# Full-height operands in a convolution's transforms, split products with the late part last, and a transposition moved one block on

## The chip, the core and the metric

The kernel runs on one core of a Trainium2 chip. The core has five engines with an instruction stream each: TensorE (PE) multiplies matrices of up to 128 rows into PSUM, VectorE (DVE) and ScalarE (ACT) work element by element, GpSimd (POOL) works element by element more slowly and issues gathers, and SyncE (SP) issues most DMA transfers. Streams run in order and wait for each other by semaphores. The metric is the device time of one launch in microseconds (us); less is better. What is shown of a kernel's inside comes from one profiled execution. "PEld" is TensorE's loading of the stationary operand, which precedes each product.

## The reference

One encoder layer on 512 tokens of width 1024, in float32, batch 1:

```python
def rmsnorm(x, g): ...                     # x / rms(x) * g
h = x + hybrid_mixer(rmsnorm(x))
h = h + peer_ffn(rmsnorm(h))
out = rmsnorm(h)
```

The mixer projects the normed tokens to ten blocks of 1024 columns and runs two branches. Branch A is a gated linear recurrence (HGRN2) over 8 heads, forward and backward, each head with a 128 x 128 state: `S_t = diag(f_t) S_{t-1} + k_t v_t^T, o_t = S_t^T q_t`, then a norm and an output gate. Branch B is a convolution:

```python
def bidirectional_fftconv(u, h_fwd, h_bwd, bias):
    L = u.shape[1]                         # 512
    kern = jnp.concatenate([h_fwd, jnp.zeros_like(h_fwd[:1]), h_bwd[1:][::-1]], axis=0)
    uf = jnp.fft.rfft(u, n=2 * L, axis=1)
    kf = jnp.fft.rfft(kern, n=2 * L, axis=0)
    return jnp.fft.irfft(uf * kf[None], n=2 * L, axis=1)[:, :L] + u * bias
```

with `u = v * x1` behind a short convolution of width 3, and `h_fwd`, `h_bwd` made by a small network of positions, `sin(...) @ filt_w3`, times a decaying window. Both branches are projected, gated, added and projected again. The channel mixer (PEER) forms 8 queries of 256 values a token, scores them against two sets of 128 sub-keys each, takes the 16 best of the sums, and for these 16 of 16,384 experts a head adds `softmax * gelu(x . u_e) * v_e`.

## The kernel before

**Split products.** Products that need accuracy are made from two parts of each operand, a high part (a cast to the type fp32r on ACT) and a low part (source minus high part, on DVE or POOL): `split`, lines 83 to 86. `mm3` (L89 to L95) then issues three products for each pair of 128-row blocks: high x high (L93), high x low (L94) and low x high (L95), block after block. In the rows of the profile, `whi`, `wlo` are a weight block's parts, `xh`, `xl` those of the normed tokens, `uh`, `ul` those of a row of the experts' table; the first operand of `mm3` is the stationary one. The low part is made from the high part, so it is there last.

**Order.** The code is written against a layer that records instructions, finds their dependencies, and then lists each engine's instructions by its own schedule of costs and readiness. The written order sets priorities; `issue_after` adds an edge. `weave(main, fill, per)` advances `fill` by a step each time the numbers that `main` yields have summed to `per`.

**Stages.** Norm and transposition of the tokens (to about 20 us); the convolution, `hyena`; its projection with gates; the recurrence, `hgrn`; output projections; queries and selection of experts (`queries`, `select`, `gates_out`); the expert loop (`rows`).

**Convolution.** Channels go in four passes of 256. A pass projects `x1`, `v`, `x0` for two blocks of 128 channels, forms `u`, folds it about its middle row into a sum and a difference (`sd`) and transposes these (L439). The middle row, one value per channel, is brought over by a product with one output row (L444): `pm[:1] = uj[:, H].T @ ident`. The FFTs are products with cosine and sine matrices: `ft` (L393 to L399) makes two blocks with `mm3` and adds the middle row by one further product, `alt` times `um` or `fm` (L399). These one-row operands are tiles of 33 rows: the high part in row 0, the low part in row 32, zeros between (`one_row`, `split_row`). `nyquist` (L404 to L406) makes one row of output, and the way back adds its own one-row product (L545, `YN` and `alt`). The filter's last layer is `hid2` (128 rows: 64 high, 64 low) times `fw3h` (L470) plus 64 rows of `hid2` times `fw3l` (L471), for four blocks a pass; then window, fold and split into `f0`, `f1` on DVE and ACT.

**Recurrence.** For each head, `scores` (main) is woven with the next head's projections (`project`, four blocks of 24 products; fill) at `per` 6.0, 5.2 for the last head. `scores` makes running sums `Z` of the gates' logarithms, exponentials `E0`, `EZ`, then transposes keys (L680), multiplies them with values (L686) and adds states `S` on DVE; seven levels follow, each with two subtractions (L707, L708), an exponential on ACT (L709), three products on DVE (L710 to L712), a score product on PE (L716) and a predicated copy (L717). Between heads ACT changes tables for sigmoids and back for the logarithm `lf`, on which the next `Z` (L646) depends.

**Expert loop.** `act_row` (one of 128 blocks of experts) splits a row of the table and issues 24 products into `ps_a`; buffers for `uh`, `ul` are two each. In the loop its low part is made by POOL. `combine` accumulates into `acc`.

## Time and profile before

| | |
|---|---|
| median of 3 runs | 2172.9 us (2167.37 to 2174.68) |
| the profiled execution's own time | 2161.79 us |
| its span, first to last instruction | 2160.0 us |
| granted TensorE clock, mean | 0.991 |
| PE busy | 2087.8 us, 97% |
| DVE busy | 1721.2 us, 80% |
| ACT busy | 967.1 us, 45% |
| POOL busy | 635.4 us, 29% |

A row of a group reads: line, engine, operation, output and inputs by the program's names, stationary and moving shapes, count; then busy time, mean ns of one, and idle time of the engine just before, with what ended it. A product's shape `33*128 33x256` is a stationary operand of 33 rows and 128 columns and a moving one of 33 rows and 256 columns. In a timeline each row begins with its start and its duration in us, and brackets give idle time before it and what ended that. Products overlap in PE's pipeline, so the distance from start to start tells what one costs; its duration is longer. A float32 product (not fp32r) of the program is two records.

### The profile page before, as it was taken

What the parts mean: (1) busy time and instruction counts of PE and PEld (TensorE: products, weight loads), DVE (VectorE), ACT (ScalarE), POOL (GpSimd) and SP (SyncE); (2) the same over time, 40 slices, a digit from 0 to 9 for tenths busy, and PEclk for the clock granted to TensorE, in tenths of its full rate; (3) what the DMA queues carried; (4) which work ended last, traced back from release to release, by engine and by line L of the source; (5) the groups of instructions that cost most, each with busy time, mean ns of one, the idle gap of its engine ahead of it and who ended that gap; (6) DMA issues with size and microseconds to landing.
All of it is one profiled execution on the core that took longest, in us unless ns stands there. A gap on an engine that the chain in (4) does not pass through costs nothing.

```text
span 2160.0 us, 29749 instructions
## 1 busy us (share of the span) xinstructions
PE 2087.8 (97%) x11117; PEld 1827.0 (85%) x11117; DVE 1721.2 (80%) x3073; ACT 967.1 (45%) x1382; POOL 635.4 (29%) x361
## 2 busy tenths in 40 slices
PE   7999999999999999988989999999999999999998
PEld 6777778888888889778889899998998998998997
DVE  6777763799989664999999978878788778877874
ACT  5544442666676532235767523333333333333233
POOL 0000000000000000000000487777677677577650
PEclk9999999999999999999999999999999999999999
DMA  5212113212222263213455699888888888879864
GB/s 192 80 49 57 46 50 111 69 59 59 72 66 59 79 205 127 69 37 120 182 215 211 228 340 342 301 315 318 284 326 323 297 306 326 311 276 325 309 246 146
DMA packets 153661, 406.89 MB, mean 188 GB/s; under 512 B 12425, under 2 KB 65419, under 8 KB 151852
## 3 DMA queue, kind: packets, MB, share of 16 engines
q1 hardware_dynamic: 109884, 255.59, 35.2%
q0 software_dynamic: 36864, 134.23, 17.0%
q10 hardware_dynamic: 6768, 15.17, 2.1%
q8 instruction: 87, 1.43, 0.3%
q14 instruction: 58, 0.48, 0.1%
HBM read 372.83 MB, written 32.11 MB: 187 GB/s over the span
## 4 chain that ended last, share of the span: by engine, by line
PE 75%; DVE 16%; ACT 5%; issue 2%; DMA 1%; POOL 0%; ACTq 0%; DVEq 0%; POOLq 0%
PE acc L971 8%; PE acc L972 8%; PE acc L970 8%; PE ps_a L95 7%; PE ps_a L93 7%; PE ps_a L94 7%; PE ps_mm L94 6%; PE ps_mm L93 6%; PE ps_mm L95 6%; PE ps_g L1226 2%; DVE wlo L86 2%; PE ps_x L93 1%; PE ps_x L716 1%; PE ps_x L95 1%; PE ps_x L94 1%
## 5 line engine op out<-in xcount | busy, mean ns | idle before, releaser
L86 POOL TENSOR_TENSOR ul<-uraw,uh 128x1024 fp32r<-128x1024 f32 x100 | 263.9, 2639 | 608.0 <-DMA gt<-Gd 403.4
L95 PE MATMUL ps_a<-pxh,ul 128*128 128x384 f32 x1008 | 344.2, 342 | 10.4 <-DVE ul L86 6.9
L93 PE MATMUL ps_a<-pxh,uh 128*128 128x384 f32 x1008 | 344.2, 341 | 10.2 <-ACT gact L863 8.3
L94 PE MATMUL ps_a<-pxl,uh 128*128 128x384 f32 x1008 | 341.9, 339 | 0.0
L85 ACT CAST vh<-vraw 128x1024 fp32r<-128x1024 f32 x128 | 134.6, 1052 | 431.5 <-DMA vraw<-in_v 333.3
L972 PE MATMUL acc<-vh,gl 128*128 128x512 f32 x768 | 300.7, 392 | 0.0
L971 PE MATMUL acc<-vl,gh 128*128 128x512 f32 x768 | 300.5, 391 | 0.0
L970 PE MATMUL acc<-vh,gh 128*128 128x512 f32 x768 | 298.7, 389 | 0.0
L931 DVE SCALAR_TENSOR_TENSOR xg<-grow,gw,xg 128x1024 f32<-128x1024 f32 x127 | 206.7, 1628 | 73.0 <-DMA grow<-in_v,gidx 71.3
L922 DVE SCALAR_TENSOR_TENSOR grow<-grow,xg 128x1024 f32<-128x1024 f32 x128 | 200.5, 1585 | 75.4 <-DMA grow<-in_u,gidx 75.1
L93 PE MATMUL ps_mm<-xh,whi 128*128 128x512 f32 (+1 forms) x656 | 257.6, 393 | 3.1 <-ACT gt L238 1.4
L95 PE MATMUL ps_mm<-xh,wlo 128*128 128x512 f32 (+1 forms) x656 | 256.0, 391 | 4.2 <-DVE wlo L86 4.2
L94 PE MATMUL ps_mm<-xl,whi 128*128 128x512 f32 (+1 forms) x656 | 256.9, 392 | 0.3 <-DVE xl L194 0.3
L824 POOL IOTA iota<- 128x512 bf16 x1 | 1.2, 1235 | 791.3 <-DVE gt L279 791.3
L93 PEld LDWEIGHTS ps_a<-pxh,uh 128*128 128x128 f32 x1008 | 192.4, 191 | 15.5 <-ACT gact L863 9.4
L902 POOL DMA_INDIRECT grow<-in_u,gidx x128 | 195.4, 1527 | 32.5 <-issue 23.1
L95 PEld LDWEIGHTS ps_a<-pxh,ul 128*128 128x128 f32 x1008 | 192.1, 191 | 12.7 <-DVE ul L86 8.6
L94 PEld LDWEIGHTS ps_a<-pxl,uh 128*128 128x128 f32 x1008 | 192.3, 191 | 3.8
L85 ACT CAST whi<-wraw 128x1024 fp32r<-128x1024 f32 x112 | 117.5, 1049 | 162.9 <-PE ps_mm L94 131.4
L86 DVE TENSOR_TENSOR vl<-vraw,vh 128x1024 fp32r<-128x1024 f32 x128 | 176.3, 1380 | 12.4 <-ACT vh L85 12.2
L902 POOL DMA_INDIRECT grow<-in_v,gidx x128 | 174.7, 1365 | 37.6 <-issue 17.8
L85 ACT CAST uh<-uraw 128x1024 fp32r<-128x1024 f32 x128 | 134.5, 1051 | 99.9 <-PE ps_a L94 71.5
(413 smaller groups left out, 4260.7 us busy)
## 6 DMA issues: line engine op xcount, KB each, us to landing
uraw<-in_uT SPq DMA_DIRECT2D x128, 512.0 KB, 6.5
vraw<-in_v SPq DMA_DIRECT2D x128, 512.0 KB, 5.6
wraw<-in_w_in SPq DMA_DIRECT2D x80, 512.0 KB, 3.6
Gd<-Gs SPq DMA_DIRECT2D x12, 2048.0 KB, 7.3
gt<-Gd SPq DMA_DIRECT2D x32, 768.0 KB, 8.9
wraw<-in_w_q SPq DMA_DIRECT2D x16, 512.0 KB, 3.7
wraw<-in_w_b SPq DMA_DIRECT2D x8, 512.0 KB, 3.6
wraw<-in_w_a SPq DMA_DIRECT2D x8, 512.0 KB, 4.0
```

The source lines that it names most:

```text
L85: nc.scalar.copy(hi, src)
L86: return (eng or nc.vector).tensor_sub(lo, src, hi).ins
L93: nc.tensor.matmul(out, ah, bh, start=(i == 0), stop=False)
L94: nc.tensor.matmul(out, ah, bl, start=False, stop=False)
L95: nc.tensor.matmul(out, al, bh, start=False, stop=(stop and i == n - 1))
L902: nc.gpsimd.indirect_dma_start(out=t, out_offset=None, in_=tab, in_offset=bass.IndirectOffsetOnAxis(ap=gidx[:, j : j + 1], axis=0))
L922: nc.vector.scalar_tensor_tensor(t, t, 1.0, xg, op0=ALU.mult, op1=ALU.mult, accum_out=gdot[:, j : j + 1])
L931: nc.vector.scalar_tensor_tensor(gacc, t, gw[:, j : j + 1], gacc, op0=ALU.mult, op1=ALU.add)
L970: nc.tensor.matmul(acc[k][:, c], gh[:, ts_], vh[:, ds_], start=(r == 0), stop=False)
L971: nc.tensor.matmul(acc[k][:, c], gh[:, ts_], vl[:, ds_], start=False, stop=False)
L972: nc.tensor.matmul(acc[k][:, c], gl[:, ts_], vh[:, ds_], start=False, stop=(r == NK - 1))
L1226: nc.tensor.matmul(pg[:, q * P : q * P + P], own[:, q], rows[:, q], start=True, stop=True)
```

## The change

Three edits, all of order or shape; the result is the same sum of products, but for the low part of the filter's last layer, which now multiplies both halves of `hid2`.

1. The one-row operands and `alt` are tiles of 128 rows, zero outside rows 0 and 32; `fw3l` has 128 rows, with the low part in both halves; the middle row comes over by a transposition of 128 columns, of whose output row 0 is used.
2. `mm3` issues, for all blocks, high x high and one mixed product, and then, for all blocks, the other mixed product: with the stationary operand's low part, or, in `ft` (`late=1`), with the moving operand's. The high part of the stationary operand is thereby last used after 16 of 24 products.
3. In `scores` the number yielded ahead of the key transpositions is 4.0 for 3.5. With the 2.0 before it, the sum reaches 6.0 there, so the first of the four projection blocks is written ahead of the transpositions (before, behind the first states).

Lines of the changed kernel are two higher from L96 on: L399 becomes L401, L680 becomes L682. `mm3`'s products are L94, L95 and L97.

```diff
-def mm3(nc, out, terms, stop=True):
+def mm3(nc, out, terms, stop=True, late=0):
     n = len(terms)
     for i, ((ah, al), (bh, bl)) in enumerate(terms):
         nc.tensor.matmul(out, ah, bh, start=(i == 0), stop=False)
-        nc.tensor.matmul(out, ah, bl, start=False, stop=False)
-        nc.tensor.matmul(out, al, bh, start=False, stop=(stop and i == n - 1))
+        nc.tensor.matmul(out, *((al, bh) if late else (ah, bl)), start=False, stop=False)
+    for i, ((ah, al), (bh, bl)) in enumerate(terms):
+        nc.tensor.matmul(out, *((ah, bl) if late else (al, bh)), start=False, stop=(stop and i == n - 1))
...
     def one_row(name):
-        t = cp.tile([LOW + 1, HC], F32R, name=name)
+        t = cp.tile([P, HC], F32R, name=name)
         nc.vector.memset(t.bitcast(F32), 0.0)
...
-    alt = cp.tile([LOW + 1, H + 2], F32R, name="alt")
+    alt = cp.tile([P, H + 2], F32R, name="alt")
...
-        nc.vector.memset(raw[: LOW + 1, : H + 2], 0.0)
+        nc.vector.memset(raw[:, : H + 2], 0.0)
...
-        nc.scalar.copy(alt, raw[: LOW + 1, : H + 2])
+        nc.scalar.copy(alt, raw[:, : H + 2])
...
-        mm3(nc, dst, [((mh[:, t, sl], ml[:, t, sl]), (src[0][:, t], src[1][:, t])) for t in range(2)], stop=mid is None)
+        mm3(nc, dst, [((mh[:, t, sl], ml[:, t, sl]), (src[0][:, t], src[1][:, t])) for t in range(2)], stop=mid is None, late=1)
...
             pm = psum(P)
-            nc.tensor.matmul(pm[:1], uj[:, H : H + 1], C.ident, start=True, stop=True)
+            nc.tensor.transpose(pm, uj[:, H : H + P], C.ident)
             split_row(um[:, js], pm[:1])
...
-        fw3l = w2.tile([FH, 2, HC], F32R, name="fw3l", bufs=1)
+        fw3l = w2.tile([2 * FH, 2, HC], F32R, name="fw3l", bufs=1)
         with tc.issue_after(C.turned):
             nc.scalar.copy(fw3h, fw3)
-        nc.vector.tensor_sub(fw3l, fw3[:FH], fw3h[:FH])
+        nc.vector.tensor_sub(fw3l, fw3, fw3h)
...
-            nc.tensor.matmul(ps, hid2[:FH, t * P : t * P + P], fw3l.rearrange("f d c -> f (d c)"), start=False, stop=True)
+            nc.tensor.matmul(ps, hid2[:, t * P : t * P + P], fw3l.rearrange("f d c -> f (d c)"), start=False, stop=True)
...
         nc.vector.tensor_mul(E0, KQ[:, 1:3], E0)
-        yield 3.5
+        yield 4.0
```

## The prediction

> **What bounds the kernel now.** I read the page first, for which engine the end hangs on:
>
> ```profile
> PE 2087.8 (97%) x11117; PEld 1827.0 (85%) x11117; DVE 1721.2 (80%) x3073; ACT 967.1 (45%) x1382; POOL 635.4 (29%) x361
> ...
> PE 75%; DVE 16%; ACT 5%; issue 2%; DMA 1%; POOL 0%; ACTq 0%; DVEq 0%; POOLq 0%
> ```
>
> TensorE (PE) has three quarters of the chain, but that is a mean over stages. So the second view is the sums by window. Columns: window, its length, then busy time (and instruction count) of PE, PEld, DVE, ACT and POOL, the granted clock, DMA.
>
> ```profile
> 92.60:147.20 54.60, 50.99 (x279) 39.44 (x277) 42.33 (x91) 26.17 (x54) 0.00 (x0) 1.00 0.14 44
> 472.00:514.00 42.00, 40.73 (x230) 34.30 (x229) 38.43 (x67) 27.31 (x34) 0.00 (x0) 1.00 0.22 63
> 900.00:1183.00 283.00, 252.78 (x1590) 233.85 (x1589) 276.84 (x929) 171.39 (x285) 0.00 (x0) 0.95 0.39 141
> 1205.00:1216.00 11.00, 7.43 (x26) 7.12 (x27) 11.00 (x42) 4.44 (x7) 7.06 (x2) 0.69 0.65 215
> 1216.00:2160.00 944.00, 936.33 (x4655) 841.91 (x4654) 737.31 (x684) 325.03 (x411) 624.52 (x353) 1.00 0.84 298
> ```
>
> The convolution (30 to 345 us, four passes; the first row is the window of it in which PE is least busy) has PE busy for 50.99 of 54.60 and VectorE (DVE) for 42.33, 78%: PE sets its pace. One head of the linear recurrence takes 42.0 us and both engines are nearly full. Selection (900 to 1183) is DVE's, 276.84 of 283. The expert loop from 1216 is PE's, 99% busy: what comes before it only shifts it.
>
> **Part 1: height and the transposed row.** Third view: PE's instructions in order of time around one product of 33 rows (start, duration).
>
> ```profile
> 221.93 0.28 PE L95 MATMUL ps_x<-f1h,sol 128*128 128x256 f32 x1
> 222.14 0.38 PE L399 MATMUL ps_x<-fm,alt 33*128 33x256 f32 x1
> 222.45 0.39 PE L93 MATMUL ps_x<-f0h,coh 128*128 128x256 f32 x1
> 222.68 0.28 PE L94 MATMUL ps_x<-f0l,coh 128*128 128x256 f32 x1
> 222.80 0.28 PE L95 MATMUL ps_x<-f0h,col 128*128 128x256 f32 x1
> ```
>
> Products of full height start 0.12 us apart (222.68 to 222.80). Across the 33-row one, three steps take 0.75 us (221.93 to 222.68) instead of 0.36: it costs 0.39 us beyond an equal product, half on entering and half on leaving. "Busy" hides that, since nothing waits on a semaphore. The groups by line count such products (count, then busy us and mean ns):
>
> ```profile
> L471 PE MATMUL ps_x<-fw3l,hid 64*128 64x512 f32 x16 | 7.9, 494 | 0.0
> L470 PE MATMUL ps_x<-fw3h,hid 128*128 128x512 f32 x16 | 7.6, 477 | 0.1
> L399 PE MATMUL ps_x<-um,alt 33*128 33x256 f32 x16 | 6.1, 381 | 0.0
> L399 PE MATMUL ps_x<-fm,alt 33*128 33x256 f32 x16 | 6.1, 381 | 0.0
> ```
>
> The filter pairs have a price of their own, with a step of 0.42 between products of 512 columns:
>
> ```profile
> 78.92 0.49 PE L471 MATMUL ps_x<-fw3l,hid 64*128 64x512 f32 x1
> 79.34 0.50 PE L470 MATMUL ps_x<-fw3h,hid 128*128 128x512 f32 x1
> ```
>
> So has the Nyquist chain (its first and last neighbour, six products between them):
>
> ```profile
> 102.33 0.28 PE L95 MATMUL ps_x<-f1h,sol 128*128 128x256 f32 x1
> ...
> 103.83 0.28 PE L94 MATMUL ps_x<-usl,ceh 128*128 128x256 f32 x1
> ```
>
> And the one-column product that brings the middle row over:
>
> ```profile
> 250.36 0.60 PE L439 MATMUL ps_x<-ident,sd 128*128 128x128 f32 x4
> 250.89 0.38 PE L444 MATMUL ps_x<-ident,u 128*1 128x128 f32 x2
> 251.20 0.50 PE L93 MATMUL ps_mm<-xh,whi 128*128 128x512 f32 x1
> 251.54 0.39 PE L94 MATMUL ps_mm<-xl,whi 128*128 128x512 f32 x1
> 251.77 0.40 PE L95 MATMUL ps_mm<-xh,wlo 128*128 128x512 f32 x1
> ```
>
> - L399: of 32, 24 stand between full products: 24 x 0.39 = 9.4 us. The other 8 open the Nyquist chain: from 102.33 to 103.83 are 8 steps in 1.50 us, 0.54 over 8 x 0.12. That chain keeps its one-column output (L404 to L406), whose entry and exit cost what L444's do, 0.29: from 250.36 to 251.54 are 1.18 us, against 4 transposes at 0.11 (four last 0.60, one 0.27: a step of 0.11), two records at 0.11 and a 512-column step of 0.23 (251.54 to 251.77). So 8 x 0.25 = 2.0.
> - L545, the same 33 rows, twice a pass: 8 x 0.39 = 3.1.
> - L471: a step of 0.42 (78.92 to 79.34) instead of 0.23, on entering and on leaving: 16 x 0.38 = 6.1. Its filter split on DVE stays one instruction with the same 512 elements per row.
> - L444, twice a pass: two records become one transposition of full width: 0.29 + 0.11, so 8 x 0.40 = 3.2.
>
> Together 23.8 us, 20.6 of it from height. The order shows these places: first PE in a pass's filter transforms, before and then changed (f1, f0 are the filter's halves, so and ce the trigonometric matrices, h and l high and low part).
>
> ```order
> L93 MATMUL ps_x<-f1h,soh 128x256
> L94 MATMUL ps_x<-f1l,soh 128x256
> L95 MATMUL ps_x<-f1h,sol 128x256
> L93 MATMUL ps_x<-f1h,soh 128x256
> L94 MATMUL ps_x<-f1l,soh 128x256
> L95 MATMUL ps_x<-f1h,sol 128x256
> L399 MATMUL ps_x<-fm_323,alt 128x256
> ```
>
> ```order
> L94 MATMUL ps_x<-f1h,soh 128x256
> L95 MATMUL ps_x<-f1h,sol 128x256
> L94 MATMUL ps_x<-f1h,soh 128x256
> L95 MATMUL ps_x<-f1h,sol 128x256
> L97 MATMUL ps_x<-f1l,soh 128x256 x2
> L401 MATMUL ps_x<-fm_323,alt 128x256
> ```
>
> Same products, the low part of the source last. Does PE's gain survive? If DVE could run no denser than in a head (38.43/42.00 = 0.915), the window 92.6 to 147.2 could shrink to 42.33/0.915 = 46.3, by 8.3 us; PE's saving there is about a quarter, 6. So DVE's throughput covers it; its chains may not. The table of waits (total, times, longest) has here:
>
> ```profile
> PE ps_x L93 <- ACT f0h L85: 2.0, 2, 1.8
> ```
>
> The filter's first product waits up to 1.8 us for the fold. I allow 0.5 us a pass for such waits, with PE arriving earlier: **-22**. Bounds: -24 (none), and -14 (2.5 us in each of four passes).
>
> The Trainium skill bears on this twice, against each other. Its page "TensorEngine Tiling (Array Packing)", section "Key Properties", says that a change of tiling mode drains TensorE; by it the 20.6 us go. Its page "TensorE: Matmul & The Clock Gate", section "Why this matters for your kernels", says that a product of 32 rows takes as long as one of 128; by it height is worth 0 and part 1 3.2. The trace's 0.75 against 0.36 speaks for the first.
>
> **Part 2: late parts last, and the transposition a block later, in a head.** The table of waits:
>
> ```profile
> PE ps_x L680 <- DVE EZ L670: 6.4, 7, 1.1
> ```
>
> In the order, the key transpositions (L680, in the change L682) stood behind 16 products of the head's value projection and now stand behind all 24 of a projection and the product of ones: 8 x 0.23 = 1.8 us more cover, so that wait goes, and wlo has 16 products ahead of its first use. But is PE the pace? DVE's rows between heads, with its idle time in brackets:
>
> ```profile
> 468.90 0.74 DVE L717 COPY_PREDICATED sct<-masks,ps_x 128x512 f32<-128x512 uint8 x1 [1.33 <-PE ps_x L716]
> ```
>
> ```profile
> 473.52 1.23 DVE L646 TENSOR_TENSOR_SCAN Z<-smask,lf 128x512 f32<-128x512 f32 x1 [1.21 <-ACT lf L637]
> ```
>
> Of DVE's 3.6 us of idle a head (42.00 - 38.43), 2.5 are these two, behind ScalarE's (ACT's) chain of sigmoids and logarithm; elsewhere DVE is full and PE waits for it. So a head shortens only where work of DVE moves into this hole. DVE just there, before and changed (L717 becomes L719):
>
> ```order
> L717 COPY_PREDICATED sct<-masks,ps_x 128x512
> L707 TENSOR_TENSOR Dt<-Z 128x512
> L717 COPY_PREDICATED sct<-masks,ps_x 128x512
> L708 TENSOR_TENSOR Dt<-Z 128x512
> L635 MEMSET lf 128x2
> L86 TENSOR_TENSOR wlo<-wraw,whi 128x1024
> L710 TENSOR_TENSOR KM<-KQ,Dt 128x512
> ```
>
> ```order
> L709 TENSOR_TENSOR Dt<-Z 128x512
> L710 TENSOR_TENSOR Dt<-Z 128x512
> L637 MEMSET lf 128x2
> L719 COPY_PREDICATED sct<-masks,ps_x 128x512
> L86 TENSOR_TENSOR wlo<-wraw,whi 128x1024
> L712 TENSOR_TENSOR KM<-KQ,Dt 128x512
> ```
>
> One copy of 0.74 us moves behind the last Dt, into the hole: 7 x 0.74 = 5, of which I take **-4**, since such rows overlap a little. Bounds: 0 (ACT's chain grows by as much) and -9 (PE's idle of 1.27 a head is all regained: 42.00 - 40.73, seven heads). In what the change adds, ACT's KT copy now stands between the two halves of a norm and ahead of the exponentials that feed DVE.
>
> **Part 3: entry into the expert loop.** In selection DVE is full: a product that waits less arrives at the next wait, **0**. At the loop's entry PE is idle:
>
> ```profile
> 1203.33 0.33 PE L94 MATMUL ps_a<-pxl,uh 128*128 128x384 f32 x1
> 1203.51 0.34 PE L95 MATMUL ps_a<-pxh,ul 128*128 128x384 f32 x1
> 1205.19 0.44 PE L93 MATMUL ps_a<-pxh,uh 128*128 128x384 f32 x1 [1.35 <-ACT uh L85]
> 1205.47 0.34 PE L94 MATMUL ps_a<-pxl,uh 128*128 128x384 f32 x1
> 1209.18 0.69 PE L95 MATMUL ps_a<-pxh,ul 128*128 128x384 f32 x1 [3.38 <-POOL ul L86]
> ```
>
> ```profile
> 1205.21 7.06 POOL L86 TENSOR_TENSOR ul<-uraw,uh 128x1024 fp32r<-128x1024 f32 x2 [6.41 <-ACT uh L85]
> ```
>
> The window 1205 to 1216 above does 26 products in 11.0 us; at 0.18 us each (1203.33 to 1203.51) that is 4.7, so 6.3 are lost, part of it at the granted clock of 0.69 behind the gap. With ul last, 16 products x 0.18 = 2.9 us lie between uh and ul, and ul takes POOL 7.06/2 = 3.5. ACT's order there, before and changed:
>
> ```order
> L863 ACTIVATE gact_11038<-ps_a_11013 128x384
> L85 CAST vh_11097<-vraw_11095 128x1024
> L85 CAST gh_11091<-gact_9949 128x768
> L85 CAST vh_11103<-vraw_11101 128x1024
> L863 ACTIVATE gact_11038<-ps_a_11062 128x384
> L85 CAST uh_11109<-uraw_11107 128x1024
> ```
>
> ```order
> L865 ACTIVATE gact_11038<-ps_a_11013 128x384
> L85 CAST uh_11109<-uraw_11107 128x1024
> L865 ACTIVATE gact_11038<-ps_a_11062 128x384
> L85 CAST gh_11091<-gact_9949 128x768
> L85 CAST vh_11097<-vraw_11095 128x1024
> ```
>
> The cast of uh no longer stands behind gh and two vh, so POOL starts a row earlier. With the 1.35 us, most of which lie before 1205, 7.5 are lost, less some 1.5 for later rows: **-6** (bounds -8 and 0: SP asks for two more uraw ahead of the vraw and gt). Counted in the whole order, 152 instead of 168 ps_a products lie between the last gates product and the first combine: 16 x 0.18 = 2.9, of which I take **-2** (0 to -3). In the loop itself the same 24 products a row remain, and nothing waits: 0.
>
> **Sum:** -22 - 4 - 6 - 2 = **-34 us** against the profiled execution (span 2160.0, its time 2161.8), so about 2128. The median of the runs shown is 2172.9, 11 above that execution; I subtract from the median: **2139 us**. Bounds summed: -14 to -44, so 2129 to 2159; some 4 more below for the spread of the runs, 2167.37 to 2174.68.
>
> **Rivals.**
> 1. *The pace passes on.* ACT and DVE chains take back part 1 to its bound -14, heads give 0, the entry keeps its waits, the rows give -2: -16, **2157 us**. For it: the 1.8 us wait for f0h, DVE at 91% in a head. Against: DVE's room of 8.3 in the tightest window.
> 2. *Height costs nothing.* The long steps come from something else about these operands (one row freshly written by DVE, say), and a full-height product takes them too: 3.2 from L444, then 4 + 6 + 2: -15, **2158 us**. Against: L471's operand fills 64 rows, isn't fresh, and costs the same 0.39.
> 3. *Slower: ACT's queue in a head.* KT's copy needs the transpositions behind 24 products; behind it on ACT wait the exponentials, and DVE's KM rows for those. In the head shown the block starts and ACT comes to the norm here:
>
> ```profile
> 477.64 0.48 PE L93 MATMUL ps_mm<-xh,whi 128*128 128x512 f32 x1
> ```
>
> ```profile
> 487.56 0.69 ACT L113 ACTIVATE hrs<-ps_x,epsc 128x512 f32<-128x512 f32 x1 [0.19 <-PE ps_x L742]
> ```
>
> 24 x 0.23 from 477.64 end at 483.2, with ones and transpositions at some 484.7: 2.9 us to spare. It decides once the block ends later than that, and the kernel is slower by more than 0.3% once a head loses (30 + 6.5)/7 = 5.2 us. At 5.5: -30 + 38.5 = +8.5, **2181 us**. Against: the waits that would delay the block are those moved behind it.
>
> **How the numbers follow.** Forecast 0.74, rivals 1 to 3: 0.16, 0.05, 0.05. What a measurement here can tell is 0.3%, 6.5 us. Faster by more: nearly all of the first three, less a slice where two of them fall short: 0.90; within: 0.05; slower: 0.05. Range 2124 to 2160: it holds the forecast's own and both rivals that end faster, and leaves out the slower one and the edges.
>
> **What would show it.** Right: L401 and L547 near 0.28 us instead of 0.38, L472 and L473 near 0.39, followers alike; the conv stage some 22 us shorter with PE idle there no more than 7; a head near 41.4 with DVE's holes smaller by one copy; no second window of clock below 0.9 at the loop's entry. Wrong: products of full height that keep 0.38, a head of 42 or more, a PE wait for f0h or wlo in each pass above 2.5 us, or ACT rows KT with idle ahead of them.

## The result, and the profile after

The changed kernel takes **2137.98 us** (median of 4, 2133.38 to 2140.67) beside 2172.6 for the kernel before on the same chip (median of 4, 2167.37 to 2174.68): a ratio of **0.9842**, 95% interval 0.9818 to 0.9866. The forecast was 2139, range 2124 to 2160. Timed again later beside the kernel before, the ratio was 0.9857 (0.9834 to 0.9879).

So the sum of -34 came out right. Its parts did not. The same places in the two profiled executions, in us from the start:

| place | before | changed | shift |
|---|---|---|---|
| convolution's last one-row product (`alt`, `YN`) ends | 310.80 | 280.20 | -30.6 |
| head 0, first L655 (now L657) | 394.87 | 365.37 | -29.5 |
| head 7, the same | 686.70 | 651.74 | -35.0 |
| last product of the gates ends | 1182.93 | 1143.31 | -39.6 |
| first combine (first product into `acc`) | 1219.82 | 1175.26 | **-44.6** |
| 500 products of combine later | 1426.18 | 1391.28 | -34.9 |
| 2000 products of combine later | 2057.87 | 2034.42 | -23.4 |
| end | 2160.02 | 2138.90 | **-21.1** |

Up to the first combine 44.6 us are won, 10 more than forecast for the whole kernel; the expert loop gives 23.5 back. The profiled execution before (2161.79) was shorter than each of the four timed ones, the changed kernel's (2140.67) was the longest of its four, so this pair differs by 21.1 where the medians differ by 34.6; where the other executions of the kernel before spend their 5 to 13 us more was not profiled.

**The convolution.** The sums by window of the stage, before and then changed (columns as in the prediction):

```profile
30.00:310.80 280.80, 276.54 (x1431) 217.19 (x1429) 208.36 (x412) 127.29 (x240) 0.00 (x0) 1.00 0.22 64
```

```profile
30.00:280.20 250.20, 250.03 (x1429) 213.61 (x1428) 206.11 (x411) 127.97 (x241) 0.00 (x0) 1.00 0.23 72
```

PE's busy time fell by 26.5, its idle time from 4.26 to 0.17: no product waits there any more. In the changed kernel's timeline the one-row product is a step like any other, ahead of the Nyquist chain too:

```profile
99.42 0.40 PE L97 MATMUL ps_x<-f1l,soh 128*128 128x256 f32 x2
99.66 0.28 PE L401 MATMUL ps_x<-fm,alt 128*128 128x256 f32 x1
99.78 0.28 PE L406 MATMUL ps_x<-f0h,altc 128*1 128x256 f32 x1
99.89 0.28 PE L407 MATMUL ps_x<-f0l,altc 128*1 128x256 f32 x1
...
100.24 0.28 PE L408 MATMUL ps_x<-fm,alt 128*1 128x256 f32 x1
100.36 0.28 PE L94 MATMUL ps_x<-ush,ceh 128*128 128x256 f32 x1
```

From 99.66 to 100.36 are six steps in 0.70 us. Products with one output column enter and leave at the full pitch of 0.12. The groups by line:

```profile
L472 PE MATMUL ps_x<-fw3h,hid 128*128 128x512 f32 x16 | 6.5, 404 | 0.1
L473 PE MATMUL ps_x<-fw3l,hid 128*128 128x512 f32 x16 | 6.4, 401 | 0.0
...
L401 PE MATMUL ps_x<-fm,alt 128*128 128x256 f32 x16 | 4.5, 280 | 0.0
```

**The heads.** Waits of PE and of DVE (total, times, longest) in six heads of the kernel before, 434.72 to 686.70:

```profile
PE ps_x L680 <- DVE EZ L670: 5.3, 6, 0.9
PE ps_mm L95 <- DVE wlo L86: 2.2, 6, 0.6
...
DVE sct L717 <- PE ps_x L716: 8.0, 6, 1.3
...
DVE ksum L651 <- ACT KQ L633: 2.2, 6, 0.4
DVE hrs L745 <- ACT hrs L114: 1.8, 6, 0.3
DVE KQ L638 <- ACT so L634: 1.5, 6, 0.3
```

And in the same six heads of the changed kernel, 403.42 to 651.74:

```profile
PE ps_x L688 <- ACT KT L684: 3.9, 5, 0.9
...
DVE sct L719 <- PE ps_x L718: 4.9, 6, 1.3
DVE ksum L653 <- ACT KQ L635: 4.2, 3, 1.5
```

The windows of six heads, before and changed:

```profile
434.72:686.70 251.98, 244.47 (x1371) 206.00 (x1370) 230.68 (x397) 163.85 (x198) 0.00 (x0) 1.00 0.21 63
```

```profile
403.42:651.74 248.32, 244.18 (x1370) 206.60 (x1369) 231.04 (x401) 161.61 (x199) 0.00 (x0) 1.00 0.21 66
```

PE's waits for `EZ` and `wlo` are gone; a new one stands behind ACT's copy of the keys. DVE idles 17.28 us instead of 21.30, which to 0.4 us is what the heads are shorter by. But its hole at the predicated copy did not close by a copy. Two DVE rows of the changed kernel show why (the last subtraction into `Dt` starts at 514.28):

```profile
515.36 0.75 DVE L719 COPY_PREDICATED sct<-masks,ps_x 128x512 f32<-128x512 uint8 x1 [0.39 <-PE ps_x L718]
...
519.82 0.75 DVE L719 COPY_PREDICATED sct<-masks,ps_x 128x512 f32<-128x512 uint8 x1 [1.31 <-PE ps_x L718]
```

The copy that moved (515.36) stands ahead of the last `KM` products; the hole opens behind these (the last ends at 518.51), until PE has made its product from them. In three of the six heads 1.25 to 1.31 us of it remain. In the other three a wait of 1.2 to 1.5 us for ACT's `KQ` stands in its place, the 4.2 above. What went are the small waits for `hrs`, `ksum` and `KQ`, 0.9 us a head before.

**The entry of the loop.** PE in order of time, then ACT:

```profile
1163.95 1.55 PE L97 MATMUL ps_a<-pxh,ul 128*128 128x384 f32 x8
1169.40 0.49 PE L94 MATMUL ps_a<-pxh,uh 128*128 128x384 f32 x1 [3.90 <-ACT gact L865]
1169.69 0.52 PE L95 MATMUL ps_a<-pxl,uh 128*128 128x384 f32 x1
```

```profile
1165.29 0.83 ACT L85 CAST gh<-gact 128x768 fp32r<-128x768 f32 x1 [7.58 <-DVE gact L959]
1166.03 1.04 ACT L85 CAST vh<-vraw 128x1024 fp32r<-128x1024 f32 x1
1166.98 1.04 ACT L85 CAST uh<-uraw 128x1024 fp32r<-128x1024 f32 x1
1167.92 1.04 ACT L85 CAST vh<-vraw 128x1024 fp32r<-128x1024 f32 x1
1168.87 0.48 ACT L865 ACTIVATE gact<-ps_a 128x384 f32<-128x384 f32 x1
```

The wait for `ul` has given way to one for a gelu (`gact`), which stands on ACT behind a cast `gh` that waits 7.58 us for DVE. Steps of 0.32 us behind it instead of 0.18 are the lower clock again (granted 0.83 in the window 1165 to 1175).

**The loop.** The page's groups of the changed kernel:

```profile
L85 ACT CAST vh<-vraw 128x1024 fp32r<-128x1024 f32 x128 | 134.7, 1053 | 597.5 <-DMA vraw<-in_v 525.0
L94 PE MATMUL ps_a<-pxh,uh 128*128 128x384 f32 x1008 | 343.9, 341 | 23.6 <-ACT gact L865 23.4
```

ACT waits 525 us in sum for loads of `vraw`; in the loop before it was

```profile
ACT vh L85 <- DMA vraw<-in_v: 327.2, 82, 10.9
```

PE waits 23.4 us for the gelu that stands on ACT behind that cast, 17.6 of them in the loop, in 13 waits. Before, the table of waits has nothing for PE behind the first combine.

### The profile page after: what moved, and what is told of

Same layout as the page of the kernel before. It is cut to its first block, busy times and chain, and to the rows that moved or that the text cites. A ratio compares the mean times of both kernels' runs of the same rounds, so it can differ in the third digit from the quotient of the medians.

```text
span 2138.9 us, 29773 instructions
## 1 busy us (share of the span) xinstructions
PE 2061.9 (96%) x11109; PEld 1819.3 (85%) x11109; DVE 1697.0 (79%) x3073; ACT 962.4 (45%) x1382; POOL 617.1 (29%) x361
## 4 chain that ended last, share of the span: by engine, by line
PE 56%; DVE 20%; DMA 9%; issue 7%; ACT 4%; POOL 3%; DVEq 0%; ACTq 0%; POOLq 0%; SPq 0%
PE ps_mm L97 7%; PE ps_mm L95 7%; PE ps_mm L94 7%; PE acc L973 5%; PE acc L974 4%; PE acc L972 4%; PE ps_a L94 4%; PE ps_a L97 4%; PE ps_a L95 4%; DMA grow<-in_u,gidx 3%; DMA vraw<-in_v 3%; DMA grow<-in_v,gidx 2%; PE ps_g L1228 2%; POOL grow L904 2%; PE ps_x L718 2%
## 5 line engine op out<-in xcount | busy, mean ns | idle before, releaser
L86 POOL TENSOR_TENSOR ul<-uraw,uh 128x1024 fp32r<-128x1024 f32 x100 | 257.6, 2576 | 634.2 <-DMA uraw<-in_uT 396.4
L94 PE MATMUL ps_a<-pxh,uh 128*128 128x384 f32 x1008 | 343.9, 341 | 23.6 <-ACT gact L865 23.4
L95 PE MATMUL ps_a<-pxl,uh 128*128 128x384 f32 x1008 | 342.3, 340 | 0.0
L933 DVE SCALAR_TENSOR_TENSOR xg<-grow,gw,xg 128x1024 f32<-128x1024 f32 x127 | 194.9, 1534 | 88.6 <-DMA grow<-in_v,gidx 87.5
L94 PE MATMUL ps_mm<-xh,whi 128*128 128x512 f32 (+1 forms) x656 | 259.4, 397 | 1.6 <-ACT xh L195 1.3
L924 DVE SCALAR_TENSOR_TENSOR grow<-grow,xg 128x1024 f32<-128x1024 f32 x128 | 189.4, 1497 | 88.5 <-DMA grow<-in_u,gidx 88.5
L95 PE MATMUL ps_mm<-xl,whi 128*128 128x512 f32 (+1 forms) x656 | 255.2, 390 | 0.3 <-DVE xl L196 0.3
L94 PEld LDWEIGHTS ps_a<-pxh,uh 128*128 128x128 f32 x1008 | 191.1, 190 | 34.1 <-ACT gact L865 30.8
L97 PE MATMUL ps_a<-pxh,ul 128*128 128x384 f32 x1008 | 200.9, 340 | 10.7 <-DVE ul L86 10.3
L86 DVE TENSOR_TENSOR vl<-vraw,vh 128x1024 fp32r<-128x1024 f32 x128 | 188.9, 1477 | 18.9 <-ACT vh L85 18.8
L904 POOL DMA_INDIRECT grow<-in_u,gidx x128 | 185.8, 1451 | 45.3 <-issue 22.4
L95 PEld LDWEIGHTS ps_a<-pxl,uh 128*128 128x128 f32 x1008 | 191.1, 190 | 3.2
L97 PEld LDWEIGHTS ps_a<-pxh,ul 128*128 128x128 f32 x1008 | 177.7, 190 | 12.9 <-DVE ul L86 12.3
L974 PEld LDWEIGHTS acc<-vh,gl 128*128 128x128 f32 x768 | 144.1, 188 | 30.2
L973 PEld LDWEIGHTS acc<-vl,gh 128*128 128x128 f32 x768 | 144.1, 188 | 28.9 <-DVE vl L86 0.8
```

Of the source, the lines that this page charges most:

```text
L86: return (eng or nc.vector).tensor_sub(lo, src, hi).ins
L94: nc.tensor.matmul(out, ah, bh, start=(i == 0), stop=False)
L95: nc.tensor.matmul(out, *((al, bh) if late else (ah, bl)), start=False, stop=False)
L97: nc.tensor.matmul(out, *((ah, bl) if late else (al, bh)), start=False, stop=(stop and i == n - 1))
L904: nc.gpsimd.indirect_dma_start(out=t, out_offset=None, in_=tab, in_offset=bass.IndirectOffsetOnAxis(ap=gidx[:, j : j + 1], axis=0))
L924: nc.vector.scalar_tensor_tensor(t, t, 1.0, xg, op0=ALU.mult, op1=ALU.mult, accum_out=gdot[:, j : j + 1])
```

## Experiments

All time ratios are against the kernel before on the same chip; "loop" is the time from the first combine to the end in the profiled execution, 940.2 before and 963.6 changed.

### Each part alone

Part 1 alone: 128 rows for the one-row operands, `alt` and `fw3l`, and the transposition.

```diff
-        t = cp.tile([LOW + 1, HC], F32R, name=name)
+        t = cp.tile([P, HC], F32R, name=name)
...
-        fw3l = w2.tile([FH, 2, HC], F32R, name="fw3l", bufs=1)
+        fw3l = w2.tile([2 * FH, 2, HC], F32R, name="fw3l", bufs=1)
...
-            nc.tensor.matmul(pm[:1], uj[:, H : H + 1], C.ident, start=True, stop=True)
+            nc.tensor.transpose(pm, uj[:, H : H + P], C.ident)
```

> The kernel before with part 1 alone: one-row operands and filter layer of 128 rows, the middle row by a transposition; order of products and head as before. Theory (the steps around products of 33 and 64 rows are a cost of PE's own, and PE paces the convolution): the convolution's last product ends 22 to 28 us earlier than before, L399 near 0.28 us, and the 1.8 us wait for f0h on PE stays, since the order of products is the old one; heads, queries and entry of the expert loop keep their lengths; time about 2148, 2143 to 2153. Rival (the gain of 30.6 us in the convolution came mostly from the late parts multiplied last, and height passes its pace on to the fold and ScalarE): convolution 10 to 15 us shorter, time about 2160.

Measured: 2146.78 us, ratio 0.9911 (0.9892 to 0.9930); convolution 24.5 us shorter, six heads 251.98 us as before, so as the theory has it. The loop takes 947.4, 7 us more than before, with no edit in it.

The order of the three products alone (`mm3`, and `late=1` in `ft`):

```diff
-        nc.tensor.matmul(out, ah, bl, start=False, stop=False)
-        nc.tensor.matmul(out, al, bh, start=False, stop=(stop and i == n - 1))
+        nc.tensor.matmul(out, *((al, bh) if late else (ah, bl)), start=False, stop=False)
+    for i, ((ah, al), (bh, bl)) in enumerate(terms):
+        nc.tensor.matmul(out, *((ah, bl) if late else (al, bh)), start=False, stop=(stop and i == n - 1))
```

> The kernel before with the new order of the three products alone (late parts last, the transforms with the moving operand's low part last); heights and head as before. Theory: the convolution ends 3 to 8 us earlier, because the waits for f0h and wlo go but every step around 33 and 64 rows stays at 0.39; heads up to 2 us shorter in all; 8 to 10 us less between the last product of the gates and the first combine; time about 2157 to 2163. If the expert loop's 23 us of give-back in the changed kernel is caused by the new order of a row's products, the loop from first combine to the end is some 960 us here too, and the time about 2175 to 2185. Rival (order makes the convolution's gain): convolution 15 us or more shorter.

Measured: 2169.83 us, ratio 1.0010 (0.9989 to 1.0030). The convolution is 5.8 us shorter and the first combine comes 16.8 earlier, but the loop takes 966.1: all of it is given back. The theory's convolution (3 to 8 us) holds, and so does its condition for the loop (some 960 us); the time lies between the two that it gave.

The key transpositions alone:

```diff
-        yield 3.5
+        yield 4.0
```

> The kernel before with the key transpositions one projection block later, nothing else. Theory (VectorE paces a head, and a copy into the hole behind ScalarE's logarithm is all that is won): a head of 41.5 instead of 42.0, 4 us over seven heads, time about 2168. Rival A (the waits of PE on the transpositions, 6.4 us in all, are the price and all of it comes back): 6 us or more, 2165 or less. Rival B (the predicated copy moves only with the new order of products too): nothing, 2172.

Measured: 2167.25 us, ratio 1.0007 (0.9995 to 1.0018). The six heads take 250.36 instead of 251.98, less than half of the theory's 4 us in seven; in the time nothing shows. DVE's hole at the copy was not smaller in it (11.5 us in six heads; 8.0 before).

The convolution splits cleanly. The windows of part 1 alone, and of the order alone:

```profile
30.00:286.30 256.30, 250.70 (x1419) 212.24 (x1419) 205.52 (x410) 125.25 (x239) 0.00 (x0) 1.00 0.23 69
```

```profile
30.00:305.00 275.00, 274.47 (x1423) 216.68 (x1422) 205.90 (x411) 127.54 (x237) 0.00 (x0) 1.00 0.22 66
```

Height took 25.8 us off PE's busy time and left its idle time (5.60; 4.26 before). The order left the busy time within 2.1, of which about half are products that now stand behind the mark, and took the idle time away (0.53). Together -24.5 - 5.8 = -30.3, against -30.6 measured: the two add up. To the convolution's very last product, a few steps behind the mark, it is -24.7, -5.3 and -30.3; profiles of kernels with the same convolution end it up to 1.7 us apart.

In the heads each edit alone passes most of the wait on. PE's waits in six heads, with the order alone, and with the transpositions alone (before: 5.3 for `EZ` and 2.2 for `wlo`):

```profile
PE ps_x L682 <- DVE EZ L672: 6.5, 6, 1.2
```

```profile
PE ps_mm L95 <- DVE wlo L86: 5.3, 8, 1.2
```

Each alone is worth 1.6 us in six heads, both 3.7 (251.98 to 248.32).

### Which height is free

The changed kernel with 65 rows instead of 128 in the one-row operands and `alt`:

```diff
-        t = cp.tile([P, HC], F32R, name=name)
+        t = cp.tile([65, HC], F32R, name=name)
...
-    alt = cp.tile([P, H + 2], F32R, name="alt")
+    alt = cp.tile([65, H + 2], F32R, name="alt")
```

> The changed kernel with one-row operands and alt of 65 rows instead of 128; the filter layer keeps 128. Theory (TensorE pays for a product whose height falls in another class than its neighbours', 33 and 64 rows alike at 0.38 us, and 65 rows count as full): L401 and L547 near 0.28 us, three steps across one 0.36 to 0.40 us, convolution as in the changed kernel, its last product some 280 us after the start. Rival (any height below 128 costs, or the cost goes with the rows that are missing): L401 at 0.33 to 0.38 us, and the convolution 5 to 18 us longer than the changed kernel's.

Measured (one execution, 2145.21 us, its loop 967.6): the convolution's last one-row product ends at 278.64, and the group reads

```profile
L401 PE MATMUL ps_x<-fm,alt 65*128 65x256 f32 x16 | 4.5, 283 | 0.0
```

Three steps across such a product take 0.36 us in the median of 32, 0.35 with 128 rows, 0.74 with 33. So what costs is not the missing rows: 33 and 64 rows cost the same 0.39 us, 65 and 128 nothing.

With that the trace agrees with the Trainium skill ("TensorEngine Tiling (Array Packing)", "Key Properties"), by which a change of tiling mode drains TensorE: its section "Tiling Modes" knows row tiles of 32, 64 and 128, and if the height picked the smallest that holds it, 33 and 64 rows would fall under 64, and 65 under 128. That the height picks the mode is an inference; no run shows the mode itself. What the Trainium skill says in "TensorE: Matmul & The Clock Gate", "Why this matters for your kernels", equal time for 32 rows and 128, does not hold for 33 rows here beside products of full height: 0.74 us over three steps against 0.35.

### Where the loop's time goes

The changed kernel again, and four variants of the loop's rows. "Steady" rows are those behind the entry.

The changed kernel itself:

> The changed kernel itself, timed beside the kernel before on the same chip as the next three. Reading so far: it reaches the first combine 44.6 us earlier than before and gives some 10 to 24 us back in the expert loop. Time 0.984 of before, with before at 2166 to 2173; in its profile the loop from first combine to the end is 958 to 968 us, with PE waiting ten times or more for ScalarE's gelu (gact), and ScalarE above 500 us for vraw. Rival (the give-back was chance of one execution): loop 940 to 950 in this profile, time 2128 or less.

Measured: 2137.49 us, 0.9857 (0.9834 to 0.9879), loop 961.5; ACT waits 516.7 us for `vraw`, PE eight times, 12.8 us, for `gact`. So the give-back is not chance of one execution.

The old order of products in every row of the experts (`mm3_pairs` is `mm3` as it was before), all else as changed:

```diff
-        mm3(nc, pa[:, :ND], [((uh[:, k], ul[:, k]), (xh[:, k, T0 : T0 + ND], xl[:, k, T0 : T0 + ND])) for k in range(KB)])
+        mm3_pairs(nc, pa[:, :ND], [((uh[:, k], ul[:, k]), (xh[:, k, T0 : T0 + ND], xl[:, k, T0 : T0 + ND])) for k in range(KB)])
```

> The changed kernel, but a row of the expert loop issues its 24 products block after block as before. Theory 1 (the loop's length, 940 us in the profile before and 964 in the profile after, follows when the gathers land, whatever the order of a row's products): time within 3 us of the changed kernel's 2138, plus up to 6 us at the loop's entry, where PE again waits for ul; so 2138 to 2145, and the loop between 940 and 965 in its profile. Theory 2 (products with the late part last hold uh longer or take ul later, and so make the loop slower): the loop back to 940, time about 2120.

Measured: 2132.41 us, 0.9846 (0.9829 to 0.9863), loop 948.1. The loop is some 15 us shorter, but the first combine comes 5.9 later (1181.13), and by ratio it equals the changed kernel: between the two theories.

Old order in the steady rows only:

```diff
-        mm3(nc, pa[:, :ND], [((uh[:, k], ul[:, k]), (xh[:, k, T0 : T0 + ND], xl[:, k, T0 : T0 + ND])) for k in range(KB)])
+        (mm3_pairs if steady else mm3)(nc, pa[:, :ND], [((uh[:, k], ul[:, k]), (xh[:, k, T0 : T0 + ND], xl[:, k, T0 : T0 + ND])) for k in range(KB)])
```

> The changed kernel, with the rows of the expert loop behind its entry in the old order of products, block after block; the rows before and at the entry keep the late part last. Theory (the new order costs the loop: uh is released after 16 of 24 products, ScalarE runs ahead to the next vh and stands there for vraw with gelu behind it): first combine as early as in the changed kernel, loop 940 to 950 us, PE at most three waits for gact, 10 to 20 us faster than the changed kernel on the same chip, so 0.975 to 0.980 of before. Rival (the loop's length is chance): the same time as the changed kernel within 3 us.

Measured: 2128.36 us, 0.9820 (0.9796 to 0.9845), loop 945.4; 9.1 us faster than the changed kernel on the same chip, a little less than the theory's 10 to 20.

The kernel before, with the new order in the steady rows only (`mm3_late` is the changed `mm3`):

```diff
-        mm3(nc, pa[:, :ND], [((uh[:, k], ul[:, k]), (xh[:, k, T0 : T0 + ND], xl[:, k, T0 : T0 + ND])) for k in range(KB)])
+        (mm3_late if steady else mm3)(nc, pa[:, :ND], [((uh[:, k], ul[:, k]), (xh[:, k, T0 : T0 + ND], xl[:, k, T0 : T0 + ND])) for k in range(KB)])
```

> The kernel before, with only the rows of the expert loop behind its entry in the new order of products; all else as before. Theory: slower than before by 15 to 25 us, the loop some 960 to 966 us, with PE waits for gact and ScalarE above 500 us behind vraw. Rival (chance, or a matter of when the loop begins): within 4 us of before.

Measured: **2180.12 us**, 1.0058 (1.0039 to 1.0077), loop 959.1. ACT's and PE's waits in its loop:

```profile
ACT vh L85 <- DMA vraw<-in_v: 534.5, 95, 14.1
```

```profile
PE ps_a L103 <- ACT gact L874: 13.1, 10, 3.6
```

So the new order of a row's products, alone, makes the loop slower, by 13 us in the medians (the theory had 15 to 25). ScalarE and GpSimd have the same order of instructions in both kernels, SyncE differs in three places, VectorE in the place of `vl` and of `gl`.

A third order in the steady rows, which holds `uh` to the last product:

```diff
+    for i, ((ah, al), (bh, bl)) in enumerate(terms):
+        nc.tensor.matmul(out, ah, bh, start=(i == 0), stop=False)
+    for i, ((ah, al), (bh, bl)) in enumerate(terms):
+        nc.tensor.matmul(out, al, bh, start=False, stop=False)
+        nc.tensor.matmul(out, ah, bl, start=False, stop=(stop and i == n - 1))
```

> The changed kernel, with the rows of the expert loop behind its entry in a third order: eight products of high by high, then in turn low by high and high by low, so that uh is in use until the last of the 24 products and ul is needed from the ninth. It tells the early release of uh from the late use of ul. Theory (early release of uh): loop 940 to 950 us, as fast as the variant with old loop rows. Rival A (late use of ul, which keeps ul's buffer): loop in between, since ul is needed later than in the old order. Rival B (neither): 958 to 968 as in the changed kernel.

Measured: 2144.06 us, 0.9897 (0.9866 to 0.9928), loop 964.1, with PE waiting for `ul` (14.3 us) and not for `gact`. It settles nothing: the scheduler also moved 95 of ACT's instructions in it.

**How `vraw` goes round.** SP, ACT and DVE of the changed kernel, where PE then waits 2.41 us:

```profile
1599.14 0.33 SPq L940 DMA_DIRECT2D vraw<-in_v  x1
1602.48 0.33 SPq L844 DMA_DIRECT2D uraw<-in_uT  x1
1615.18 2.61 SPq L940 DMA_DIRECT2D vraw<-in_v  x2
```

```profile
1601.29 1.05 ACT L85 CAST vh<-vraw 128x1024 fp32r<-128x1024 f32 x1 [4.33 <-DMA vraw<-in_v]
1607.21 1.05 ACT L85 CAST vh<-vraw 128x1024 fp32r<-128x1024 f32 x1 [4.87 <-DMA vraw<-in_v]
...
1621.62 1.04 ACT L85 CAST vh<-vraw 128x1024 fp32r<-128x1024 f32 x1 [11.31 <-DMA vraw<-in_v]
1622.57 1.04 ACT L85 CAST uh<-uraw 128x1024 fp32r<-128x1024 f32 x1
1623.51 0.48 ACT L865 ACTIVATE gact<-ps_a 128x384 f32<-128x384 f32 x1
```

```profile
1608.57 1.23 DVE L924 SCALAR_TENSOR_TENSOR grow<-grow,xg 128x1024 f32<-128x1024 f32 x1 [0.84 <-DMA grow<-in_u,gidx]
...
1613.94 1.22 DVE L86 TENSOR_TENSOR vl<-vraw,vh 128x1024 fp32r<-128x1024 f32 x1
```

```profile
1624.05 0.69 PE L94 MATMUL ps_a<-pxh,uh 128*128 128x384 f32 x1 [2.41 <-ACT gact L865]
```

`vraw` has two buffers. The cast of 1601.29 is done at 1602.34, but its buffer is free only when DVE has made `vl` from it, at 1615.16, behind products of gathered rows (L924) that themselves wait for gathers. SP, with nothing issued since 1602.48, at once issues the next load (and at 1617.46, behind the next `vl`, the one after it); it is there for the cast of 1621.62, and that cast, the next `uh`, the gelu and then PE follow one after the other. From issue to landing such a load takes 5.7 us in the median:

```profile
vraw<-in_v SPq DMA_DIRECT2D x108, 512.0 KB, 5.7
```

Worked out from the starts and ends of loads, casts and `vl` (means of rows 31 to 114), and from the starts of the products into `acc`, in us:

| kernel | load issued to `vh` starts | `vh` starts to `vl` ends | first 500 products of combine | 500 to 2000 | rest |
|---|---|---|---|---|---|
| before | 7.01 | 8.16 | 206.4 | 631.7 | 102.2 |
| changed, old order in steady rows | 6.88 | 8.18 | 211.5 | 631.7 | 102.1 |
| changed, old order in all rows | 6.90 | 8.36 | 206.6 | 639.4 | 102.1 |
| before, new order in steady rows | 6.12 | 9.22 | 211.3 | 644.7 | 103.2 |
| before, new order everywhere | 6.36 | 9.00 | 219.2 | 644.7 | 102.2 |
| changed | 6.34 | 8.94 | 216.0 | 643.1 | 104.5 |
| changed, second profile | 6.38 | 8.92 | 216.9 | 641.5 | 103.1 |

From the 500th product to the 2000th 631.6 or 631.7 us are PE's own pace: five of the profiles have it, two of the rows above and the three kernels with the place of `vl` moved, below; the transpositions alone have 632.2, part 1 alone 633.8, the third order 637.2. With the new order in the steady rows it is 641.5 to 645.5 in five profiles (the kernel with 65 rows is the fifth): **10 to 14 us** more, the size of the two differences of medians, 9.1 and 13.3. The next load of `vraw` goes out 0.03 us after the end of `vl` in every kernel, the one before too, so the first two columns are one round of a buffer, which serves two rows. Before, a load had 7.0 us; with 6.1 to 6.4 it has the 5.7 of its landing and little more, and what the wait for `vl` adds is then added to the row; this last step is argued from the means.

PE's own waits in this stretch, counted from the traces, tell the same: none in the five profiles with 631.6 or 631.7, and 5.8 to 9.5 us, in three to seven waits for `gact`, in the five with the new order. Behind some of these the granted clock falls too: to 0.50 from 1623.64 to 1627.04 in the changed kernel, in and behind the wait of 2.41 us above, where a product lasts 0.69 us instead of 0.34. The old order in all rows has 4.0 us of waits, 2.3 for `ul` and 1.7 for `gact`, and takes 639.4: a loss of 7.7 us there without the new order, whose cause stays open.

The first 500 products tell of the entry: the kernels whose first combine comes early by the new order at the entry need 5 to 13 us more for them (though part 1 alone, with the old entry, needs 3.9 more and the kernel before with new steady rows 4.9). The variant with old steady rows starts its 500th at 1388.3, the one with old rows everywhere at 1387.7. Of the entry's gain nothing is left there.

Then `vl` was put earlier on VectorE, with the products of the changed kernel: `vls` holds the subtractions that make `vl`, and a gathered row's product may not go ahead of the last but one.

```diff
-        split(nc, vh, vl, raw)
+        vls.append(split(nc, vh, vl, raw))
...
-            nc.vector.scalar_tensor_tensor(t, t, 1.0, xg, op0=ALU.mult, op1=ALU.mult, accum_out=gdot[:, j : j + 1])
+            with tc.issue_after(vls[-2]):
+                nc.vector.scalar_tensor_tensor(t, t, 1.0, xg, op0=ALU.mult, op1=ALU.mult, accum_out=gdot[:, j : j + 1])
```

> The changed kernel with an edge on VectorE alone: in the expert loop a product of a gathered row (L924, L933) may not go ahead of the low part vl of the table row written two before it. In the order that puts each vl 2.5 such products earlier than in the kernel before; in the changed kernel it is 0.4 later than before (51 of 128 stand behind one more). The order of TensorE's products stays that of the change. Theory A (what costs the loop is VectorE's place for vl: it frees vraw's buffer, whose load ScalarE waits for): loop 945 us or less, time 0.975 to 0.980 of before, ScalarE below 400 us behind vraw. Theory B (the cost is the row's own order of products, with uh free after 16 of 24): loop 956 to 966, time 0.984 to 0.988 as the changed kernel.

Measured: **2124.62 us, 0.9800 (0.9774 to 0.9825)**, loop 946.0, with 631.6 us from the 500th to the 2000th product; `vh` start to `vl` end takes 2.74 us instead of 8.94. ACT's waits in its loop:

```profile
ACT vh L85 <- PE acc L977: 185.2, 56, 3.6
...
ACT vh L85 <- DMA vraw<-in_v: 60.3, 14, 15.4
```

The theory that names VectorE's place for `vl` holds here, by time and by wait. ACT now waits for PE, and for the load only 60 us of 525. PE has one wait in the loop, 4.0 us for `ul` at 1232, among the first 500 products, which take 212.2.

The same edge on the variant with old steady rows:

> The variant with the late part last everywhere but in the expert loop behind its entry (0.982 of before), with the same edge on VectorE as in the run before this one. Theory A: loop shorter than 945 us, 940 or less, time 0.975 to 0.980. Theory B, or vl early enough as it is: loop 940 to 948, time 0.980 to 0.983. If vl ahead of the gathered rows holds back the gathers' buffers instead: loop above 950 and time above 0.984.

Measured: 2126.80 us, 0.9807 (0.9782 to 0.9832), loop 949.8, again 631.6 in the middle; its first 500 products take 216.1, so that the loop is longer than either theory put it. With `vl` early the order of a row's products makes no difference that the intervals show.

Last, the kernel before with `vl` a little later: it is recorded one row later and behind a product of a gathered row, so that the order of TensorE, ScalarE and GpSimd stays as it was.

```diff
-        split(nc, vh, vl, raw)
+        nc.scalar.copy(vh, raw)
+        pend.append((vl, raw, vh))
...
+                with tc.issue_after(stts[-3]):
+                    nc.vector.tensor_sub(*args)
```

> The kernel before, with the order of TensorE, ScalarE and GpSimd unchanged, in which 40 of the 128 low parts vl stand behind one (three of them, at the loop's start, behind two to six) more products of gathered rows on VectorE, 0.37 on average; the new order of a row's products gives 0.40, with one each for 51. It tells VectorE's place for vl from the new order of products itself. Theory A (that place is the whole cause): slower than before by 8 to 20 us, loop above 950 us, ScalarE above 450 us behind vraw, PE waits for gact. Theory B (the products' order, with uh free earlier, is needed for the loss, and the edge of the run with vl early only made up for it): within 4 us of before, loop 940 to 947.

Measured: 2165.36 us, 0.9993 (0.9981 to 1.0005), loop 942.4, 631.6 in the middle. Theory A falls in its strict form: the place on VectorE alone does not make the loss. `vl` ends 8.71 us after `vh` starts, the load has 6.32, and the ring holds: PE has no wait in the middle. With the new order of products, and about the same place, the first is 8.9 to 9.2: between the end of `vh` and the start of `vl` DVE idles 0.97 us a row before, 1.38 here, and 1.74 and 1.82 in the kernel before with the new order in the steady rows and in the changed kernel, mostly for gathers. Why the gathers come later there stays open; that `uh` is free after 16 products, so that ScalarE and GpSimd run at other times, was only argued. Shown is that the new order in the steady rows makes the loss, that it comes with a longer wait for `vl`, and that an earlier `vl` takes it away.

## Why the prediction was right, and where not

- **Part 1, height: right in cause, term a little too small.** The fall of PE's busy time was put at 20.6 us for height and 3.2 for the transposition; part 1 alone took 25.8 off in its window, and 25.4 when the same products are counted from the start of the span. The missing 1.6 to 2.0 is the Nyquist chain: 0.29 were kept for each of 8 chains (2.3 us) by analogy with L444, a plain float32 product, and the changed trace shows none. (Between the two rows that the prediction shows of it stand seven products, not six; its eight steps are right.) The transposition's 0.40 holds: from the first of four transpositions to the second product behind the group are 1.18 to 1.26 us before and 0.84 to 0.87 in the changed kernel.
- **-22 for the convolution: the wrong sign of a term.** An allowance of 0.5 us a pass was taken off for waits with PE arriving earlier. The table of waits has 4.2 us of them in the stage before, the 2.0 for `f0h` that the prediction quotes and

```profile
PE ps_mm L95 <- DVE wlo L86: 1.7, 2, 1.4
PE ps_mm L93 <- ACT whi L85: 0.5, 1, 0.5
```

The late-last order removes them, and it was counted as nothing in this stage: -5.8 alone. PE's idle time there was forecast at no more than 7; it is 0.17.
- **Part 2, heads: -4, measured -3.7 in six, -5.5 from head 0 to head 7. The number is right, the path is not.** That a head shortens by what DVE idles less was right. But the hole at the copy did not take in a copy, as the rows above show; the small waits went instead, and why they went was not followed. The prediction also put the 1.33 us there behind ACT's chain, while its own row names PE's product. So the agreement in size is luck. That `EZ`'s wait goes with the transpositions moved was right; alone, that only put a wait for `wlo` in its place. Of the 2.9 us to spare on ACT nothing was left: in the head from 486.17 to 527.79 the norm starts there at 493.61, and the first transpositions end at 493.90. PE waits up to 0.9 us a head for the copy of the keys, which stands on ACT behind an exponential (497.72, behind one from 496.76); rival 3 had it the other way round, and its 5.2 us a head are far off.
- **Part 3, entry: -8 was not kept.** From the last gates product to the first combine are 32.0 us instead of 36.9, so -4.9. The 16 products are not saved but moved ahead of the last gates product (544 instead of 528 stand there), into the stage that DVE sets. Of the two waits together, 4.73, 3.90 remain, now for `gact`; that no second window of clock below 0.9 would be left was wrong (0.83). The step forgot what stands ahead of a gelu on ACT: `gh`, which waits for DVE. And by the 500th product of combine the kernel stands where it stood at head 7, -34.9.
- **Selection at 0: also off.** From the first to the last product of the gates take 182.9 us before, 182.6 with the old order in all rows and 179.8 to 180.2 in every profile with the new order there. So about 2.9 us were won where DVE was taken to be full; by which wait stays open.
- **The loop at 0: the step that failed.** "In the loop itself the same 24 products a row remain, and nothing waits" looked at PE alone. In the pair the loop is longer by 9.6 us in the first 500 products, 11.4 in the steady part and 2.3 at the end. The order of the products changed when other engines wait, in a loop where ACT already waited 327.2 us for `vraw`. From the table the ring of two `vraw` buffers had, by an estimate, about 1 us of room in 15: 7.0 us for a load before, 6.1 to 6.4 where rows got longer. It is no sharp bound, since the last kernel above held with 6.32.

That the total came out right was luck. In the profiled pair 10.6 us more than forecast were won up to the first combine, most of it the convolution's surplus of 8.6, and the loop put at 0 lost 23.5. The pair thus gives 21.1, not 34; the medians give 34.6, because the executions of the kernel before that were timed took 5 to 13 us more than the profiled one. Rival 2 (height costs nothing) is refuted by part 1 alone. Rival 1 (the pace passes on) did not happen in the convolution, where DVE's and ACT's chains followed; its idea, that a gain ends in the next queue, holds for the entry and the loop. Rival 3 did not come.

## What to carry to other kernels

Count the products whose height falls into another class than their neighbours' and pad their operands with zeros: here each cost 0.39 us though "busy" showed PE full, and 65 rows were enough for the one-row operands (one execution). An order that is good where the late operand is the wait may harm where nothing waits: before applying it everywhere, add up for every ring of buffers the load, the wait for the engine that frees it and its work, and hold that against the rows that the buffers cover. Here two buffers and 15 us for two rows had about 1 us to spare (the estimate above), and with one ordering edge on VectorE the changed kernel took 0.9800 of the time before, where it took 0.9842 and 0.9857 without it.

## What the runs showed that was not expected

- A product of 65 rows costs what one of 128 does; products with one output column among full ones keep the pitch of 0.12 us (six steps in 0.70), unlike the plain float32 one, L444. Why that one paid stays open.
- In the loop the next load of `vraw` follows the end of `vl` after 0.03 us (the median of every kernel, the kernel before too), though PE is 99% busy there: a buffer can be taken the moment it is free, row after row, and not show on PE.
- A stage with the same instructions can take longer by the granted clock. Between the output projection and the queries, the kernel with only the transpositions moved and the kernel before:

```profile
836.95:856.52 19.57, 16.02 (x113) 15.40 (x111) 7.07 (x9) 7.09 (x12) 0.00 (x0) 0.83 0.54 188
```

```profile
837.99:854.31 16.32, 13.80 (x113) 13.18 (x112) 6.98 (x9) 7.00 (x12) 0.00 (x0) 1.00 0.63 204
```

The same 113 products take 16.02 us at a granted clock of 0.83 and 13.80 at 1.00; PE idles 3.55 us of the first window and 2.52 of the second. In this profile that took the heads' small gain away. What sets off the lower clock was not tried.
